# Moving the mLSTM's projections into the RWKV stage and running both scan halves beside the mLSTM

## The chip, the cores and the metric

The kernel runs on one core of a Trainium2 chip. The core's engines are TensorE (PE in the profile; its weight loads are listed apart as PEld), VectorE (DVE), ScalarE (ACT) and GpSimd (POOL); SyncE (SP) only issues transfers. The program gives each engine a queue of instructions of its own. The metric is the device time of one execution in microseconds (us). Lower is better.

## The reference

Two layers of a diffusion transformer work on 1280 tokens (256 of context, 1024 latent) of 1024 features. Each layer modulates a normalised input by vectors of a conditioning input, runs a mixer, projects its output back and ends with an MLP of 4096 hidden features. The change is in the mixer of the first ("even") layer, which joins an mLSTM and an RWKV-7 recurrence:

```python
mod = (silu_c @ ada_w[l] + ada_b[l])[:, None, :]
...
hj = jnp.concatenate([modulate(rmsnorm(xc, norm_g[l, 0]), shc_a, scc_a),
                      modulate(rmsnorm(x, norm_g[l, 0]), sh_a, sc_a)], axis=1)
...
mq, mk, mv, mo, mg, rfeat = split_cols(hj @ w_in, EV_SIZES)
qk = two_seq(lambda t: centred_dwconv(t, ml_conv), jnp.concatenate([mq, mk], axis=-1), n_ctx)
...
hm = mlstm_chunkwise(z(hd(q, ML_DIM)), z(hd(k, ML_DIM)), z(hd(mv, ML_DIM)), z(ig_fw, ig_bw), z(lf_fw, lf_bw))
y_ml = head_rmsnorm(dir_merge(hm, B, n_ctx), ml_norm) * jax.nn.sigmoid(mo.astype(f32))
rfeat = two_seq(lambda t: t + (neighbour_mean(t) - t) * rw_mu, rfeat, n_ctx)
r, k, v, wl, al, gl = split_cols(rfeat, (...))
...
y = rwkv7_scan(z(r), z(decay[0], decay[1]), z(key_d[0], key_d[1]), z(v), z(-kk), z(icl[0], icl[1]))
y_rw = y.reshape(B, T, RW_WIDTH) * (jax.nn.sigmoid(gl.astype(f32)) @ rw_g2)
out = jnp.concatenate([y_ml, y_rw], axis=-1).astype(dt)
```

`mq`, `mk` (512 features each) go through a convolution over three tokens; `mv` and `mo` (512 each) are the mLSTM's values and output gates; `mg` are 16 gate columns. `rfeat` are 1920 RWKV features, each mixed with its two neighbours in time. Both recurrences run forwards and backwards, and the two directions are added.

## The kernel before

All matmuls of projections are made of three with split operands (`mm3`, lines 288 to 291: high x high, low x high, high x low), eight along the contraction, so 24 for a run of up to 512 columns. `wsplit` (line 278) loads a block of weights on SP (line 283), copies its high part on ScalarE (284) and makes the low part on VectorE or GpSimd (285).

The order of work is written with generators. `weave` runs several of them in rounds; a number beside each says how many steps it makes per round, and generators given as `behind` go along without being waited for. What is emitted sooner has priority, and the compiler puts each engine's queue into order from that and from the data.

The even layer has these stages:

1. Start: the input is normalised and transposed; the first group of modulation vectors is computed (`ada`, line 227: 16 weight tiles per group, matmul at 246). `hh` and `hl` keep the modulated input, transposed, in two parts.
2. `lowrank` for both halves of the tokens, then `rkv(0, 0)`: projections of RWKV features through `project` (734). It copies each PSUM run to `praw` (746), scales a second copy (747) and adds the neighbours on VectorE (751, 752).
3. Eight iterations over (feature tile, half): `prepare` of one (decays, keys, chunk matrices `AR` and `BK`, lines 799 to 926) woven at rate 3 with `rkv` of the next at rate 1. `behind` them run `inverses` (inverses of 32x32 blocks on GpSimd, 771 and 772) and `joins` (two products per block pair, 671 and 678, written by 683). In the eighth iteration no `rkv` is left, and `conv` projects and convolves the 8 features of `mq` and `mk` (699 to 720).
4. Scan half 0 (`scan(0, d)`, two of the four feature tiles, both directions), woven at rate 1 with `dense` at 0.45, and `adas` behind at 0.85. `dense` (947 to 986) projects `mv`, `mo` and `mg` by token tiles: 4 column blocks of 260 by 10 token tiles; its outputs go by GpSimd's queue to memory. `adas` computes the other five groups of modulation vectors of both layers.
5. The mLSTM's gates (1194 to 1275): a chain of small instructions on all engines, written out before the next weave.
6. Scan half 1 at rate 1, the mLSTM of both directions (`mlstm`, 1287 to 1378) at 1.1, the rest of `adas` at 1.5, then `outs` (the output projection, which starts when both mLSTM directions are over and, tile by tile, when the scans have passed), then the norms ahead of the MLP.

A scan step handles 128 tokens in two half-steps of 64. Each goes through TensorE and back four times: the old state's part of the right side (1089, 1090; copied by 1092), the product with the inverse (1097; copied by 1099 on VectorE and 1100 on ScalarE), the state's update (1108, 1109; 1111 to 1117) and the output (1128, 1130). `amat` makes the chunk matrices of the next step in between (1037, 1055). `finish` (1150 to 1171) normalises a tile that both directions have passed.

Later, in the odd layer, twelve feature tiles are projected by `od_run` (the loop starts at line 1458).

Of the kernel before, what the change touches and what calls it, by code (L numbers as in the profile page):

```python
# [17 lines left out]
P = 128  # L18
D = 1024
KD = 8  # L20
# [16 lines left out]
    ("qn", 2), ("kvn", 1),  # L37
# [13 lines left out]
def host_pack(i):  # L51
# [6 lines left out]
        _cols(f["rw_ln_b"][0]), _cols(f["hg_lb"]), _cols(f["mla_q_norm"][0]), _cols(f["mla_kv_norm"][0]),  # L58
    ], axis=1)

    grow = np.zeros((4, 2, P, 512), np.float32)
    for l in range(2):
        for w, (col, nrow, j0) in enumerate(((2048, 1, 0), (5120, 3, 2))):
            for j in range(2):
                for v in range(2):
                    p = 32 * (j0 + j) + v
                    grow[2 * l + w, 0, p] = f["ada_b"][l, col + 512 * j: col + 512 * (j + 1)]
                    grow[2 * l + w, 1, p] = f["norm_g"][l, nrow, 512 * j: 512 * (j + 1)]
# [86 lines left out]
def _body(tc, nc, I, out, dbg, stop, es):  # L155
# [71 lines left out]
    def ada(l, pool, groups, bufs=3, tag="px"):  # L227
        for g in groups:
            ws = []

            def load(i):
                k, c0 = i % KD, 256 * (i // KD)
                w = pool.tile([P, 4, 256], F32, tag="adaw", name=nm("adaw"), bufs=bufs)
                SY.dma_start(w, I["ada_w"][l, k * P:(k + 1) * P, g * 2048:(g + 1) * 2048]
                             .rearrange("p (j c) -> p j c", j=4)[:, :, c0:c0 + 256])
                ws.append(w)
            for i in range(bufs):
                load(i)
            for hf in range(2):
                c0 = 256 * hf  # L240
                pr = ps(tag=tag)
                for k in range(KD):
                    yield
                    w = ws.pop(0)
                    for j in range(4):
                        TE.matmul(pr[32 * j:32 * (j + 1), 0:256], sc[:, k, :], w[:, j, :], start=k == 0, stop=k == KD - 1)
                    if KD * hf + k + bufs < 2 * KD:
                        load(KD * hf + k + bufs)
# [6 lines left out]
                ab = pc(f"adab{l}", 16 * g, 16).rearrange("p (j i) -> p j i", j=4)[:, :, 2 * hf:2 * hf + 2]  # L255
                mv = modT[:, l, 16 * g:16 * (g + 1), :].rearrange("p (j i) v -> p j i v", j=4)[:, :, 2 * hf:2 * hf + 2]
                for v in range(2):
                    V.tensor_tensor(mv[:, :, :, v], ptv[:, :, :, v], ab, op=ALU.add)
                if g >= 1:
                    w = g - 1  # L260
                    j0 = 0 if w == 0 else 2
                    for i, op in enumerate((ALU.add, ALU.mult)):
                        gr = pool.tile([P, 256], F32, tag="gr", name=nm("gr"), bufs=1)
                        SY.dma_start(gr, I["grow"][2 * l + w, i, :, c0:c0 + 256])
                        V.tensor_tensor(mr, mr, gr, op=op)
                    for j in range(2):
                        p0 = 32 * (j0 + j)
                        S.dma_start(grd[2 * l + w, :, 512 * j + c0:512 * j + c0 + 256], mr[p0:p0 + 2, :])
# [281 lines left out]
    mod_ = dram([T, 512], "mod_")  # L550
# [17 lines left out]
    with ExitStack() as ph:  # L568
# [4 lines left out]
        lay.enter_context(psum(ps=3, px=5))  # L573
# [3 lines left out]
        feats = [2064 + P * f for h in range(2) for f in (12, 13, 14)] + \  # L577
            [2064 + P * f for ft, h in order for f in (4 + ft, ft, 8 + ft)] + [P * f for f in range(8)]
# [53 lines left out]
        W = H + 4  # L632

        PART = (((0, 256, 1), (256, 386, 258)), ((638, 322, 0), (960, 320, 322)))
        SEG = (((0, 1, 256), (256, 258, 384)), ((0, 2, 640),))
        ZERO = ((0, 257), (642,))
        KEEP = (((0, 0, 256), (256, 0, 384)), ((0, 2, 320), (320, 0, 320)))
# [61 lines left out]
        def conv(f, wts, pool, tag):  # L699

            wh, wl = wts()
            for h in range(2):
                raw = pool.tile([P, W], F32, tag="praw", name=nm("praw"), bufs=1)
                for z in ZERO[h]:
                    V.memset(raw[:, z:z + 1], 0.0)
                for t0, n, r0 in PART[h]:
                    pt = ps()
                    for k in range(KD):
# [1309 lines left out]
```

## Time and profile before

| what | us |
|---|---|
| three runs | 4082.84, 4089.72, 4089.75 (median 4089.72) |
| the profiled execution | 4080.55 |
| its span, first to last instruction | 4078.4 |
| first scan copy (line 1092) and last | 671.1 and 1407.5 |
| first and last matmul of modulation (line 246) | 10.5 and 1019.0 |
| TensorE busy | 3720.3 (91% of the span) |
| VectorE busy | 2434.3 (60%) |
| ScalarE, GpSimd busy | 1369.7, 1401.2 (34% each) |

How to read it: the span is one execution; a row of a table by stage gives the stretch, its length, and for each engine the busy time and the number of instructions, then the granted TensorE clock as a share of full speed, the mean busy share of the 16 DMA engines, and GB/s. Matmuls overlap in the records, so a stretch with TensorE busy all the time need not have it at full pace. A row of the timeline gives start, length, engine, line, operation, tiles written and read, shape and count; in brackets stands the idle time before it and what ended it. In a row of groups the figures behind the bar are the busy time and the mean duration in ns, then the idle time ahead of it. In a row on one line or tile, three durations in ns are the least, the median and the greatest.

### The profile page before, as it was taken

How to read it: one execution, taken by the hardware profiler on the slowest of the kernel's cores; microseconds unless marked ns; L12 is line 12 of the kernel's file. 1: busy time of each engine (PE TensorE's matmuls, PEld its weight loads, DVE VectorE, ACT ScalarE, POOL GpSimd, SP SyncE). 2: the span in 40 equal slices, each digit the busy share in tenths (PEclk: the TensorE clock that was granted, in tenths of full speed). 3: DMA queues.
4: the chain of work that ended last, by engine and by line, in shares of the span. 5: the costliest groups of instructions: out<-in, count | busy, mean ns of one | idle time of the engine just before them, and what ended most of it. 6: DMA issues, size and time to landing. Idle time of an engine off the chain costs nothing. (4 is left out here: it accounts for less than half of the span.)

```text
span 4078.4 us, 68232 instructions
## 1 busy us (share of the span) xinstructions
PE 3720.3 (91%) x27052; PEld 3157.0 (77%) x27052; DVE 2434.3 (60%) x4387; ACT 1369.7 (34%) x2739; POOL 1401.2 (34%) x1404
## 2 busy tenths in 40 slices
PE   5988898998887989999999989998888979999998
PEld 3867687776776778999899979986666757888887
DVE  5587753443786545656655662228888466666665
ACT  3554422333344443221412143123343434223221
POOL 3055570111122244323433231233444445333332
PEclk7998998999797899999999999998999989999999
DMA  5456665778574442222322235222221354334332
GB/s 168 117 134 165 147 154 144 222 226 237 179 238 148 138 154 83 88 78 73 119 78 78 75 97 172 90 95 70 84 66 48 124 177 138 110 97 135 102 95 77
DMA packets 594776, 511.97 MB, mean 126 GB/s; under 512 B 161145, under 2 KB 521529, under 8 KB 594457
## 3 DMA queue, kind: packets, MB, share of 16 engines
q1 hardware_dynamic: 485928, 425.06, 35.8%
q10 hardware_dynamic: 97824, 48.28, 4.1%
q0 software_dynamic: 10704, 34.28, 2.3%
q8 instruction: 213, 3.49, 0.4%
q14 instruction: 107, 0.87, 0.1%
HBM read 391.59 MB, written 115.92 MB: 124 GB/s over the span
## 5 line engine op out<-in xcount | busy, mean ns | idle before, releaser
L284 ACT CAST wh<-raw 128x1024 fp32r<-128x1024 f32 x322 | 332.8, 1050 | 1019.6 <-PE ps L291 501.3
L291 PE MATMUL ps<-mh,wl 128*128 128x320 f32 (+3 forms) x1888 | 625.2, 331 | 5.8 <-POOL wl L285 5.7
L289 PE MATMUL ps<-mh,wh 128*128 128x320 f32 (+3 forms) x1888 | 625.8, 332 | 2.6 <-DVE acc L506 1.7
L290 PE MATMUL ps<-mh,wh 128*128 128x320 f32 (+3 forms) x1888 | 625.2, 331 | 0.7 <-POOL mh L341 0.7
L473 DVE TENSOR_TENSOR relu<-relu 128x320 f32<-128x320 f32 (+1 forms) x192 | 326.5, 1701 | 386.1 <-ACT relu L472 386.1
L285 POOL TENSOR_TENSOR wl<-raw,wh 128x1024 fp32r<-128x1024 f32 x145 | 353.8, 2440 | 585.1 <-ACT wh L284 585.1
L289 PE MATMUL ps<-wh,h1h 128*128 128x512 f32 x1152 | 450.8, 392 | 5.4 <-ACT acc L504 2.7
L506 DVE TENSOR_TENSOR acc<-ps,acc 128x512 f32<-128x512 f32 x540 | 359.1, 684 | 152.8 <-PE ps L291 150.4
L290 PE MATMUL ps<-wl,h1h 128*128 128x512 f32 x1152 | 449.7, 390 | 0.0
L291 PE MATMUL ps<-wh,h1l 128*128 128x512 f32 x1152 | 448.9, 390 | 0.0
L475 POOL TENSOR_TENSOR h1l<-relu,h1h 128x320 fp32r<-128x320 f32 (+1 forms) x192 | 206.5, 1076 | 495.4 <-DVE h1h L474 492.0
L291 PEld LDWEIGHTS ps<-mh,wl 128*128 128x128 f32 x1888 | 355.1, 188 | 27.2 <-POOL wl L285 7.0
L289 PEld LDWEIGHTS ps<-mh,wh 128*128 128x128 f32 x1888 | 355.4, 188 | 25.2 <-DVE acc L506 2.9
L290 PEld LDWEIGHTS ps<-mh,wh 128*128 128x128 f32 x1888 | 355.4, 188 | 22.2 <-POOL mh L341 1.0
L285 DVE TENSOR_TENSOR wl<-raw,wh 128x1024 fp32r<-128x1024 f32 x177 | 226.6, 1305 | 105.6 <-ACT wh L284 105.4
L289 PEld LDWEIGHTS ps<-wh,h1h 128*128 128x128 f32 x1152 | 216.7, 188 | 51.4 <-ACT acc L504 3.9
L289 PE MATMUL ps<-hh,wh 128*128 128x256 f32 (+3 forms) x736 | 241.3, 328 | 15.8 <-ACT r L747 4.9
L291 PE MATMUL ps<-hh,wl 128*128 128x256 f32 (+3 forms) x736 | 237.7, 325 | 19.6 <-DVE wl L285 19.3
L291 PEld LDWEIGHTS ps<-wh,h1l 128*128 128x128 f32 x1152 | 216.7, 188 | 45.7
L290 PEld LDWEIGHTS ps<-wl,h1h 128*128 128x128 f32 x1152 | 216.7, 188 | 43.4 <-DVE wl L285 0.2
L290 PE MATMUL ps<-hl,wh 128*128 128x256 f32 (+3 forms) x736 | 238.9, 325 | 5.4 <-POOL hl L630 5.1
L289 PEld LDWEIGHTS ps<-hh,wh 128*128 128x128 f32 x736 | 145.3, 197 | 25.2 <-issue 6.5
(536 smaller groups left out, 7916.3 us busy)
## 6 DMA issues: line engine op xcount, KB each, us to landing
raw<-in_mlp_w SPq DMA_DIRECT2D x256, 512.0 KB
adaw<-in_ada_w SPq DMA_DIRECT2D x96, 512.0 KB
raw<-in_ev_w SPq DMA_DIRECT2D x38, 512.0 KB
ard<-AR SPq DMA_DIRECT2D x32, 320.0 KB
bkd<-BK ACTq DMA_DIRECT2D x16, 640.0 KB
CM<-ard SPq DMA_DIRECT2D x80, 128.0 KB
BK<-bkd SPq DMA_DIRECT2D x40, 256.0 KB
qk<-qkd SPq DMA_DIRECT2D x20, 512.0 KB
```

The source lines that it names most:

```text
L284: S.copy(h, raw)
L285: (leng or G).tensor_tensor(l, raw, h, op=ALU.subtract)
L289: TE.matmul(o, lh, rh, start=first, stop=False)
L290: TE.matmul(o, lh, rl, start=False, stop=False)
L291: TE.matmul(o, ll, rh, start=False, stop=last)
L473: V.tensor_tensor(r_, r_, r_, op=ALU.mult)
L475: G.tensor_tensor(l_[:, t0:t0 + step], r_, a[:, t0:t0 + step], op=ALU.subtract)
L506: V.tensor_tensor(acc[i][:, cs_], pt, acc[i][:, cs_], op=ALU.add)
```

## The change

1. **Fillers.** `dense` is gone. The values (`v`), output gates (`o`) and convolved features (`c`) become 16 `filler` generators by feature tile. They are spread over the eight iterations of stage 3: 0, 1, 2, 1, 2, 1, 2 and 7. The gate columns become `gatecols`. `lowrank(1)` moves from ahead of the loop into its first iteration, beside `gatecols`. `prepare` runs at rate 1.6 in place of 3. Output gates are now kept feature-major (`mod_`).
2. **Neighbour mixing from PSUM.** `project` and the convolution share `mixed`: no copy to `praw`; ScalarE scales the middle and VectorE adds both neighbours straight from PSUM. PSUM is divided 4 and 4 in place of 3 and 5.
3. **`AR`** has two planes in place of three and is made in one instruction for all partitions; its write has three transfers in place of two.
4. **Scan.** Stages 4 to 6 become one weave: each direction runs scan half 0 and then half 1; the gates are a generator (`gates_ml`) beside it; the mLSTM waits for it and runs at 0.55, the modulation at 0.6.
5. **Modulation.** Groups 1 and 2 of the second layer move from `adas` to the loop of `od_run`, one step after each run. `ada` now loads 1024 neighbouring columns in place of 4 x 256.
6. **mLSTM's end.** The product with norm weight and output gate is made after the transposition, on VectorE (4 instructions), in place of one multiplication on GpSimd and one on VectorE before it and a copy on ScalarE after it.

```diff
-                w = pool.tile([P, 4, 256], F32, tag="adaw", name=nm("adaw"), bufs=bufs)
-                SY.dma_start(w, I["ada_w"][l, k * P:(k + 1) * P, g * 2048:(g + 1) * 2048]
-                             .rearrange("p (j c) -> p j c", j=4)[:, :, c0:c0 + 256])
+                w = pool.tile([P, 1024], F32, tag="adaw", name=nm("adaw"), bufs=bufs)
+                SY.dma_start(w, I["ada_w"][l, k * P:(k + 1) * P, c0:c0 + 1024])
...
-        lay.enter_context(psum(ps=3, px=5))
+        lay.enter_context(psum(ps=4, px=4))
...
+        fill = [("v", f) for f in range(4)] + [("o", f) for f in range(4)] + [("c", f) for f in range(8)]
+        meant = [0, 1, 2, 1, 2, 1, 2, 7]
...
+        def plain(wh, wl, t0, n):
+            pt = ps()
+            for k in range(KD):
+                mm3(pt[:, :n], wh[:, k, :], wl[:, k, :], hh[:, k, t0:t0 + n], hl[:, k, t0:t0 + n], k == 0, k == KD - 1)
+                if k == 3:
+                    yield
+            return pt
+
+        def mixed(h, wh, wl, o_, left, mid, right):
+
+            for t0, n, o0, p0, m, nl, nr in PART[h]:
+                pt = yield from plain(wh, wl, t0, n)
+                S.activation(o_[:, o0:o0 + m], pt[:, p0:p0 + m], AF.Copy, scale=mid)
+                o = o_[:, o0 + nl:o0 + m]
+                V.scalar_tensor_tensor(o, pt[:, p0 - 1 + nl:p0 - 1 + m], left, o, op0=ALU.mult, op1=ALU.add)
+                o = o_[:, o0:o0 + m - nr]
+                V.scalar_tensor_tensor(o, pt[:, p0 + 1:p0 + 1 + m - nr], right, o, op0=ALU.mult, op1=ALU.add)
+                yield
+
+        def filler(y, f):
+
+            wh, wl = weights()
             for h in range(2):
...
+                o_ = ep.tile([P, H], F32, tag="fo", name=nm("fo"), bufs=2)
+                if y == "c":
+                    yield from mixed(h, wh, wl, o_, *[cw[:, j, f:f + 1] for j in range(3)])
+                    by_tile(qkd[5 * h:5 * h + 5, :, f, :], o_)
+                    continue
+                for c0, nn in ((0, 3), (3, 2)):
+                    w = slice(c0 * P, (c0 + nn) * P)
+                    pt = yield from plain(wh, wl, H * h + c0 * P, nn * P)
+                    if y == "o":
+                        S.activation(o_[:, w], pt[:, :nn * P], AF.Sigmoid)
+                        yield
+                        continue
+                    S.copy(o_[:, w], pt[:, :nn * P])
...
+        def gatecols():
...
+            for t in range(NT):
+                o, tk = pt[:, 32 * t:32 * t + 32], slice(t * P, (t + 1) * P)
+                for k in range(KD):
+                    TE.matmul(o, hh[:, k, tk], gw[:, k].rearrange("p y g -> p (y g)"), start=k == 0, stop=False)
+                for k in range(KD):
+                    TE.matmul(o[:, 0:16], hl[:, k, tk], gw[:, k, 0], start=False, stop=k == KD - 1)
...
-                    for p0 in (0, 64):
-                        q = slice(p0, p0 + 64)
-                        V.tensor_tensor(to(AR[q, :, p0 // 32, w]), half_(kn)[q], dec(Wq)[q], op=ALU.mult)
+                    V.tensor_tensor(to(AR[:, :, 0, w]), half_(kn), dec(Wq), op=ALU.mult)
...
-        weave(chain(lowrank(0), lowrank(1)))
+        weave(lowrank(0))
...
-            gens = [(prepare(ft, h, cur["k"], cur["r"], cur["v"]), 3, 0)]
+            feed = [] if i else [lowrank(1), gatecols()]
             if i + 1 < len(order):
-                gens.insert(0, rkv(*order[i + 1], res))
-            else:
-                gens.insert(0, chain(*[conv(f, weights, ep, "k") for f in range(8)]))
+                feed.append(rkv(*order[i + 1], res))
+            feed += [filler(*next(fl_)) for _ in range(meant[i])]
+            gens = [chain(*feed), (prepare(ft, h, cur["k"], cur["r"], cur["v"]), 1.6, 0)]
...
-                for l, gs in ((0, (1, 2)), (1, (0, 1, 2))):
+                for l, gs in ((0, (1, 2)), (1, (0,))):
...
-        weave((dense(), 0.45, 0), (scan(0, 1), 1, 0), (scan(0, 0), 1, 0), behind=((mods, 0.85, 0),))
...
         def mlstms(d):
+            while not pre:
+                yield
...
         def scans1(d):
+            yield from scan(0, d)
             yield from scan(1, d, got[0])
...
-        weave((mlstms(1), 1.1, 0), (scans1(1), 1, 0), (mlstms(0), 1.1, 0), (mods1(), 1.5, 0), (norms0(), 3, 0), (scans1(0), 1, 0), (outs(), 1, 0))
+        weave((gates_ml(), 1, 0), (mlstms(1), 0.55, 0), (scans1(1), 1, 0), (mlstms(0), 0.55, 0), (mods1(), 0.6, 0), (norms0(), 3, 0), (scans1(0), 1, 0), (outs(), 1, 0))
...
+        mods = ada(1, epx.enter_context(tc.tile_pool(name="ad1", bufs=1, reuse_waits="tile")), (1, 2), 3, "ps")
...
                 pt = held.pop(1) if f == F0 and r in runs[:2] else od_run(w, *r)
+                next(mods, None)
```

More of the change, by code (lines that the diff above doesn't have):

```diff
@@ L549, in _body @@
     mvd = dram([T, 512], "mvd")
-    mod_ = dram([T, 512], "mod_")
+    mod_ = dram([NT, P, 4, P], "mod_")
     und = dram([640, 32, 32], "und")
@@ L576, in _body, with rw @@
         order = [(ft, h) for ft in range(4) for h in range(2)]
-        feats = [2064 + P * f for h in range(2) for f in (12, 13, 14)] + \
-            [2064 + P * f for ft, h in order for f in (4 + ft, ft, 8 + ft)] + [P * f for f in range(8)]
+        fill = [("v", f) for f in range(4)] + [("o", f) for f in range(4)] + [("c", f) for f in range(8)]
+        meant = [0, 1, 2, 1, 2, 1, 2, 7]
+        col = {"v": 1024, "o": 1536, "c": 0}
+        def rw(fs):
+            return [2064 + P * f for f in fs]
+        feats = rw((12, 13, 14)) + rw((4, 0, 8)) + rw((12, 13, 14))
+        for i, n in enumerate(meant):
+            if i + 1 < len(order):
+                ft = order[i + 1][0]
+                feats += rw((4 + ft, ft, 8 + ft))
+            at = sum(meant[:i])
+            feats += [col[y] + P * f for y, f in fill[at:at + n]]
         ready = []
@@ L736, in project @@
             wh, wl = weights()
[L737 to L752 removed]
+            yield from mixed(h, wh, wl, o_, half[:, f:f + 1], omu[:, f:f + 1], half[:, f:f + 1])
         def rkv(ft, h, res):
@@ L791, in lowrank @@
                 o_ = ep.tile([P, H], F32, tag="kn", name=nm("gg"), bufs=1)
+                g2 = ep.tile([P, 2, P], F32, tag="lr", name=nm("g2"), bufs=2)
+                SY.dma_start(g2[:, 0, :], I["rw_g2"][:, ft * P:(ft + 1) * P])
                 for t0, n in HC:
                     pt = px()
-                    TE.matmul(pt[:, :n], g2[:, ft * P:(ft + 1) * P], sgl[:, t0:t0 + n], start=True, stop=True)
+                    TE.matmul(pt[:, :n], g2[:, 0, :], sgl[:, t0:t0 + n], start=True, stop=True)
                     S.copy(o_[:, t0:t0 + n], pt[:, :n])
@@ L884, in prepare @@
                     yield
-                for p0 in (0, 64):
-                    q = slice(p0, p0 + 64)
-                    SY.dma_start(ard[d][tiles, q, ft].rearrange("c p s t -> p c (s t)"),
-                                 AR[q, :, p0 // 64:p0 // 64 + 2, :].rearrange("p c s t -> p c (s t)"))
+                SY.dma_start(ard[d][tiles, 0:64, ft].rearrange("c p s t -> p c (s t)"), AR[0:64].rearrange("p c s t -> p c (s t)"))
+                for s_ in range(2):
+                    SY.dma_start(ard[d][tiles, 64:128, ft, s_].rearrange("c p t -> p c t"), AR[64:128, :, 1 - s_, :])
                 S.dma_start(bkd[d][tiles, :, ft].rearrange("c p e s t -> p c (e s t)"), BK.rearrange("p c e s t -> p c (e s t)"))
@@ L1396, in outs @@
         def outs():
-            while over.count("m") < 2:
+            while over.count("m") < 2 or not mdone:
                 yield
@@ L1482, in _body @@
                 by_tile(fkd[d][:, :, 1, h, :], b_)
+        for _ in mods:
+            pass
         epx.close()
```

335 lines of the change are left out of this document (145 added, 190 removed).

## The prediction

> **What bounds the kernel now.** I read the page's slices first, then a table of busy times by stage, then one line of the scan by stage.
>
> ```profile
> span 4078.4 us, 68232 instructions
> PE   5988898998887989999999989998888979999998
> PEclk7998998999797899999999999998999989999999
> ```
>
> TensorE has work nearly everywhere and the clock is nearly full; the dips stand in the first 15 slices of 102 us, before the first MLP. The change edits just that stretch, so I cut it where its stages change.
>
> ```profile
> core 0: us, PE busy (x) PEld busy (x) DVE busy (x) ACT busy (x) POOL busy (x), PEclk, DMA share, GB/s
> 62.00:165.00 103.00, 85.26 (x493) 77.51 (x494) 58.32 (x92) 46.79 (x87) 20.90 (x12) 0.88 0.32 87
> 165.00:484.00 319.00, 264.96 (x1986) 227.06 (x1985) 253.09 (x418) 153.77 (x270) 151.95 (x205) 0.91 0.60 148
> 484.00:660.00 176.00, 160.99 (x1269) 150.09 (x1267) 85.14 (x140) 56.91 (x106) 96.41 (x151) 0.94 0.55 132
> 660.00:1001.00 341.00, 317.89 (x3705) 249.96 (x3705) 147.44 (x480) 108.38 (x284) 55.03 (x85) 0.92 0.78 225
> 1001.00:1054.00 53.00, 38.33 (x287) 27.73 (x285) 22.66 (x87) 17.73 (x39) 3.16 (x9) 0.55 0.52 156
> 1152.00:1287.40 135.40, 117.30 (x1320) 99.73 (x1318) 109.19 (x345) 56.38 (x208) 33.88 (x39) 0.91 0.64 194
> 1054.00:1285.00 231.00, 197.55 (x2059) 169.45 (x2057) 184.97 (x575) 96.44 (x335) 56.68 (x65) 0.91 0.66 202
> 1285.00:1465.00 180.00, 150.12 (x998) 115.25 (x999) 91.89 (x216) 79.91 (x159) 51.71 (x38) 0.84 0.45 143
> 2368.00:2580.00 212.00, 200.65 (x1297) 193.92 (x1297) 86.58 (x101) 75.21 (x151) 53.56 (x36) 0.98 0.44 133
> ```
>
> The rows are: low-rank projections; seven of the eight RWKV iterations; the eighth, with the convolutions; scan half 0 beside `dense`; the mLSTM gates; scan half 1 beside the mLSTM, first the later part and then the whole; scan half 1 beside the output projection; and far behind, the first projections of the odd layer. The two middle kinds differ. In 165 to 484 VectorE is busy 79% and TensorE 83%, a mixture in which neither is full. From 660 to 1465, 805 us, the work is a recurrence that is cut into half-steps, and `L1092` runs once per half-step and direction:
>
> ```profile
> core 0: us, DVE busy (x), PEclk, DMA share, GB/s
> 660.00:1001.00 341.00, 11.25 (x40) 0.92 0.78 225
> 1001.00:1054.00 53.00, 0.64 (x3) 0.55 0.52 156
> 1152.00:1287.40 135.40, 4.74 (x18) 0.91 0.64 194
> 1054.00:1285.00 231.00, 6.67 (x26) 0.91 0.66 202
> 1285.00:1465.00 180.00, 3.25 (x12) 0.84 0.45 143
> ```
>
> Half 0 takes 341/20 = 17.05 us a half-step, half 1 with the mLSTM 231/13 = 17.8 (135.4/9 = 15.0 once its first loads are over). The gates' 53 us hold the recurrence up almost wholly.
>
> **What the scan pays for its neighbour.** One half-step of half 0, as a whole, then `dense` in it, then the modulation:
>
> ```profile
> 908.00:925.00 17.00, 16.91 (x204) 13.65 (x206) 11.18 (x35) 7.27 (x15) 0.54 (x1) 1.00 0.83 229
> 908.00:925.00 17.00, 6.29 (x48) 5.88 (x48) 0.00 (x0) 0.00 (x0) 0.00 (x0) 1.00 0.83 229
> 908.00:925.00 17.00, 3.04 (x28) 0.93 (x32) 1.00 0.83 229
> ```
>
> TensorE looks full, but 9.3 of its 17 us are the two guests. How much lies on the path is seen in the order of time:
>
> ```profile
> 916.36 0.26 ACT L1100 COPY ZV<-ps 64x128 f32<-64x128 f32 x1 [4.53 <-DVE ZV L1099]
> ...
> 917.75 0.28 PE L291 MATMUL ps<-wt,hl 128*128 128x260 f32 x1
> 917.96 0.27 PE L1108 MATMUL ps<-ZV,KB 128*64 128x64 f32 x1
> ...
> 921.20 0.39 PE L289 MATMUL ps<-wt,hh 128*128 128x260 f32 x1
> ...
> 924.06 0.28 PE L291 MATMUL ps<-wt,hl 128*128 128x260 f32 x1
> 924.27 0.27 PE L1089 MATMUL ps<-ZV,CM 128*64 128x64 f32 x1
> ```
>
> The update `L1108` could start when `L1100` ends (916.62) and starts at 917.96: 1.3 us behind a block of `dense`. The next half-step's `L1089` waits out a whole block, 921.20 to 924.27: 3.1 us. So 4.4 of 17.05 us go with `dense`, which leaves 12.6; I take 12.7.
>
> **Part by part. Stage with the fillers (62 to 660).** Added on TensorE: eight features (values, gates) of 4 runs x 24 matmuls, 320 columns in the mean, and 160 matmuls for the gate columns, each with a load of 128 columns.
>
> ```profile
> 240.65 0.31 PE L289 MATMUL ps<-hh,wh 128*128 128x322 f32 x1
> ...
> 241.38 0.30 PE L291 MATMUL ps<-hh,wl 128*128 128x322 f32 x1
> ...
> 40.13 0.93 PEld L609 LDWEIGHTS ps<-cm,xt 128*128 128x128 f32 x8 [0.81 <-DVE xT L611]
> ```
>
> Five steps in 0.73 us give 0.146 us a matmul; eight loads in 0.93 us give about 0.113 each. Added: 768 x 0.146 + 160 x 0.113 = 112 + 18 = 130 us. The convolutions keep their 8 features. What hides the 130 is the idle part of the iterations:
>
> ```profile
> 165.00:484.00 319.00, 112.27 (x338) 66.93 (x338) 0.91 0.60 148
> ```
>
> `L289` is one of three, so 1014 projection matmuls in seven iterations: 145 each, 21 us, and the other (1986 - 1014)/7 = 139 I put at 10 us, an estimate below 139 x 0.113 = 16, since most load 64 columns and fewer. So 31 of 319/7 = 45.6 us per iteration. A filler adds 96 x 0.146 = 14. By the plan (0, 1, 2, 1, 2, 1, 2, 7 fillers, and low-rank half 1 with the gate columns in the first) TensorE needs about 75 (31 + 24 + 18), three times 45, three times 59, and in the last 10 + 98 + 12 for joins: 507. How full can it be? 83% in this row, 95% in the odd projections (200.65 of 212); with fillers always ready I take 90%: 563 us. Ahead lie the start up to about 75, one low-rank half (30) and the first projection (25). End: 693 against 660, **+33**. Bounds: at 95% +4; nothing hidden, +130. VectorE does not take over:
>
> ```profile
> L880 DVE TENSOR_TENSOR AR<-kn,Wp 64x320 f32<-64x320 f32 x64 | 41.7, 652 | 1.3 <-DMA ard<-AR 0.7
> L746 ACT COPY praw<-ps 128x256 f32<-128x256 f32 (+3 forms) x60 | 25.6, 426 | 111.9 <-DVE k L752 44.7 <-DVE r L752 24.1 <-PE ps L291 18.3
> L772 POOL TENSOR_TENSOR xu<-xu,tm 128x31 f32<-128x31 f32 (+15 forms) x155 | 112.6, 727 | 12.2
> L771 POOL TENSOR_TENSOR tm<-un,xu 128x31 f32<-128x31 f32 (+15 forms) x155 | 104.5, 674 | 37.9 <-DMA un<-und 26.1
> L683 ACTq DMA_DIRECT2D xcd<-XC x16: 366/401/754, 336.8 to 666.7; - x16
> ```
>
> `AR` is made in 32 whole pieces and not 64 halves: 21 us of VectorE go, about as much as the fillers' weight splits bring. The `praw` copies go from ScalarE; in their place VectorE now reads PSUM, so a bank comes free only when VectorE has passed, which a fourth bank eases; I cost that at nothing, and at up to 5 us an iteration if VectorE is late. The fillers' writes, two a feature, leave by ScalarE's queue, each waiting for the last pass over its tile; behind it stand the activations of `prepare`. The convolutions' writes do that already, and `dense`'s 50 small writes leave GpSimd's queue. The inverses are 217/5 = 43 us each on GpSimd; the last follows the last `prepare`, then come joins (before, the last was written at 666.7). The last iteration's 120 us cover an inverse and most joins; 15 us may show, within the bounds.
>
> **Both scan halves beside the mLSTM (660 to 1465 before).** Gone: `dense`, the serial gates, the gap between the halves. The mLSTM runs at 0.55 and not 1.1, so its 59 steps of the generator per direction last 107 rounds, after 8 for the gates: 115 of the scans' 174 rounds (87 per half). That is 26.5 of 40 half-steps; 13.5 remain. Price of a half-step in the first part: 12.7 with no neighbour, 15.0 with a full mLSTM, hence about 13.9 with half of one; 14.0 with a little modulation. VectorE's share fits: at most 147.44/20 = 7.4 us of scan and half of (109.19 - 9 x 7.4)/9 = 4.7 of mLSTM, 10 of 14. The part is 26.5 x 14.0 = 371. The rest: before, 180 us from 1285 to the MLP held 7 half-steps, the one in hand counted; 6.5 more beside weight splits alone, at 13.5, are 88. The first loads and the mLSTM's start take 20, an estimate (the mLSTM's first loads cost 231 - 13 x 15.0 = 36 in half 1). Sum 659 against 805: **-146**. Bounds: a price of 12.7 gives -180, one of 16.9 gives -50; above that the first rival holds. A new wait is the hand-over: half 1's first loads stand on SP behind half 0's last; mLSTM work covers one landing.
>
> **Modulation.** Layer 1's last two groups, 32 weight tiles, move into the odd projections, with their loads on SP and small writes on ScalarE's queue.
>
> ```profile
> 660.00:1001.00 341.00, 55.19 (x584) 13.57 (x584) 0.92 0.78 225
> L246 PE MATMUL ps<-adaw,sc x768: 376/403/637, 10.5 to 1019.4; 128*32 128x256 f32 x192
> ...
> PE ps L246 <- DMA adaw<-in_ada_w: 15.0, 5, 10.5
> ```
>
> 768 records are 96 tiles of 8; 584 are 73, at 0.76 us busy, less where matmuls overlap. 32 tiles are 24 us at most, 0 if they fell into the 11 us that TensorE is idle there. That stage is full (200.65 of 212), so I take **+17**. The od weights' loads stand behind them on SP; three buffers ahead cover a landing. The last row is of the waits up to 62 us: TensorE waits 15.0 us for such loads, 10.5 of it for the first. Whole rows of 1024 columns in place of four pieces can shorten the other 4.5: **-2**, between 0 and -4.
>
> **Sum.** -2 + 33 - 146 + 17 = -98. The profiled execution took 4080.55 us (span 4078.4), 9 under the median of the three runs, 4089.72. From it 3982.5; with half of those 9, 3987.
>
> **Rivals.** (Each with the same half of 9.)
> *The scan is paced by its own hops.* PE, VectorE and ScalarE hand each half-step on several times, in queues in order; taking `dense` away may only show other waits (in the rows above ScalarE sat 4.53 us behind VectorE's `L1099`, not behind `dense`). Place: `L1099` to `L1108`. If a half-step keeps the 17.8 of half 1 in the 33 of them that I price anew, 33 x 17.8 + 180 + 20 = 787, -18 and not -146; with 33 + 17 - 2 the kernel is 30 us slower: 4115. It decides from 16.9 us on, where 33 c + 200 is 805 - 48. For it: 17.05 and 17.8 have different neighbours and nearly one price. Against: 15.0 in the nine half-steps with a full mLSTM, where VectorE is 81% busy and so has reason to be the pace. Chance 0.11.
> *The scan runs free.* The mLSTM hides wholly: 33 x 12.7 + 180 + 12 = 611, -194, and fillers at +4: 3910. For it: `L1089` follows `dense` by 0.2 us, so it was ready. Against: VectorE is not idle. Chance 0.19.
> *A colder array.* The clock was granted 0.55 where the gates ran alone and 0.84 beside the output projection. Without `dense` the recurrence might see 0.75 and not 0.91: TensorE's 16.91 - 9.33 = 7.6 us of scan and half of (117.30 - 9 x 7.6)/9 = 5.4 of mLSTM, 10.3 a half-step, grow by 2.2, over 33 of them 72: 4059. Against it, 1054 to 1285 has no `dense` and 0.91. Chance 0.14. The Trainium skill (TensorE: Matmul & The Clock Gate, Part 1: The HAM clock gate) speaks for this rival: an idle window of some 3.4 us brings the array to half rate, and busy time brings it back. The row of 0.55 agrees; the row of 0.91 says that the mLSTM is work enough.
> *The fillers hide nothing*, since banks wait for VectorE or the order leaves them last: the first stage grows by 130, not 33: 4084, no change. For it: VectorE is 79% busy there. Against: TensorE's 17% idle. Chance 0.08.
>
> **Numbers.** Forecast 0.48, then 0.11, 0.19, 0.14, 0.08 in the order above. The range runs from 3905 (free scan) to 4075 (colder array with the fillers one fifth less hidden); the hop-paced case and most of the last stay outside. A difference under 0.2%, 8 us, cannot be told from none here. Faster 0.83, same 0.06, slower 0.11.
>
> **What would show it.** Right: scans start near 693; about 14 us between `L1092` pairs until the mLSTM ends, no hole between the halves; the MLP starts some 100 us sooner; the odd projections last about 229 us. Wrong: a clock under 0.8 in the scans, pairs over 16 us apart, scans starting after 740, or odd projections longer by over 25 us.

## The result, and the profile after

The changed kernel takes 4183.57 us (median of 4 runs, 4179.2 to 4188.22); the kernel before took 4089.12 beside it (4082.84 to 4089.75). The ratio is 1.0235, 95% interval 1.0217 to 1.0252: 94 us slower, where 103 us less was forecast and the range ended at 4075. The page of the changed kernel, by the lines with which the prediction began:

```profile
span 4178.1 us, 67908 instructions
PE   5997788888888889999999989998888879999998
PEclk7898899989888889999999999998989989999999
```

TensorE's thin part ends with slice 15 in both kernels, but from slice 4 on it no longer has a slice at 9, where it had four (6, 8, 9 and 14). Cut by stage (the columns are those of the prediction's tables), first the kernel before: filler stage, both scan stages up to the first matmul of the MLP, first projections of the odd layer, rest.

```profile
62.00:660.00 598.00, 511.21 (x3744) 454.66 (x3744) 396.54 (x648) 257.47 (x461) 269.26 (x368) 0.91 0.54 133
660.00:1494.00 834.00, 729.13 (x7153) 582.81 (x7153) 458.33 (x1374) 310.93 (x835) 175.51 (x206) 0.88 0.64 193
...
2413.00:2581.00 168.00, 159.31 (x1081) 158.33 (x1080) 56.96 (x60) 63.37 (x130) 43.75 (x26) 0.98 0.50 146
2581.00:4078.00 1497.00, 1383.56 (x9779) 1122.84 (x9777) 937.13 (x1529) 478.09 (x900) 584.76 (x546) 0.97 0.32 101
```

The same stages after the change:

```profile
59.00:840.00 781.00, 651.75 (x4774) 602.85 (x4776) 363.98 (x638) 260.14 (x444) 244.35 (x375) 0.88 0.48 119
840.00:1552.00 712.00, 595.92 (x5870) 458.55 (x5870) 421.37 (x1316) 288.11 (x773) 112.32 (x123) 0.86 0.59 182
...
2468.00:2669.00 201.00, 188.54 (x1348) 167.82 (x1346) 63.01 (x78) 64.47 (x130) 43.08 (x26) 0.97 0.67 208
2669.00:4178.00 1509.00, 1389.74 (x9777) 1128.40 (x9776) 936.72 (x1529) 479.45 (x900) 582.54 (x546) 0.96 0.32 100
```

The stage with the fillers ends at 840 and not 660 (+180). The scan stages take 712 and not 834 (-122), the odd projections 201 and not 168 (+33), the MLP 916 and not 919. The rest holds the same work and takes 1509 and not 1497; between two fixed matmuls of it (its first with `wt` and `mh`, and the last of all) lie 1479 to 1493 us in the twenty kernels of this study, so these 12 are within that scatter. The sum is 100, as the spans say. Two things stand out. TensorE is busy 141 us more in the first stage (651.75 against 511.21), and it is also idle 42 us more (129 against 87): nothing has been hidden, and something new waits. In the iterations with one filler and with two, in turn, it shows:

```profile
234.00:285.00 51.00, 46.00 (x354) 41.95 (x353) 27.09 (x53) 21.90 (x40) 9.32 (x18) 1.00 0.60 145
285.00:386.00 101.00, 74.88 (x556) 68.42 (x556) 39.34 (x62) 31.45 (x57) 36.95 (x51) 0.85 0.44 108
386.00:438.00 52.00, 49.46 (x398) 44.82 (x397) 30.55 (x57) 24.59 (x44) 15.19 (x28) 1.00 0.63 153
438.00:535.00 97.00, 70.83 (x529) 65.96 (x529) 39.18 (x61) 28.00 (x48) 57.97 (x86) 0.84 0.47 117
535.00:606.00 71.00, 57.57 (x445) 52.09 (x446) 35.45 (x62) 25.93 (x45) 18.77 (x24) 0.90 0.52 128
606.00:689.00 83.00, 64.98 (x522) 60.40 (x522) 38.19 (x71) 26.76 (x47) 40.13 (x68) 0.90 0.52 133
```

The first two iterations with one filler take 51 and 52 us, as planned (45 at 90%, 50); the first two with two fillers take 101 and 97 (66 planned), with TensorE idle for 26. The third of each kind takes 71 and 83. The timeline of the second row, on GpSimd, SP and TensorE (`L811` writes an inverse, `L662` loads it for a join, `L280` loads weights):

```profile
314.88 0.30 PE L288 MATMUL ps<-hh,wl 128*128 128x322 f32 x1
...
323.31 0.61 POOL L811 DMA_DIRECT2D xud<-xu  x1
...
326.39 0.33 SPq L662 DMA_DIRECT2D XC<-xud  x1
326.81 0.63 SPq L280 DMA_DIRECT2D raw<-in_ev_w  x1
...
332.36 0.69 PE L286 MATMUL ps<-hh,wh 128*128 128x384 f32 x1 [17.17 <-ACT wh L281]
```

SP's queue goes in order. A load that waits for an inverse stands ahead of the next weights; they leave 0.4 us after it, and TensorE, which has run out of weights, waits 17.17 us. One more wait like it comes in the next iteration with two fillers; together they are the costliest wait of TensorE between 138 and 840, where it is idle for 112 us in all:

```profile
PE ps L286 <- ACT wh L281: 33.4, 2, 17.2
```

SP's own waits in that time:

```profile
SPq L662 <- DMA xud<-xu: 141.1, 5, 34.0
SPq L659 <- PE ps L676: 50.6, 11, 9.6
SPq L280 <- DVE wl L282: 48.5, 15, 6.8
```

Five waits for an inverse, 141 us in all. The kernel before has one in this stage, 14.8 us for `xtd`.

### The profile page after: what moved, and what is told of

It is laid out like the page before. It is cut to its first block, busy times and chain, and to the rows that moved or that the text cites. A ratio compares the mean times of both kernels' runs of the same rounds, so it can differ in the third digit from the quotient of the medians.

```text
span 4178.1 us, 67908 instructions
## 1 busy us (share of the span) xinstructions
PE 3759.9 (90%) x27060; PEld 3195.6 (76%) x27060; DVE 2369.7 (57%) x4335; ACT 1351.3 (32%) x2658; POOL 1308.6 (31%) x1328
## 3 DMA queue, kind: packets, MB, share of 16 engines
q1 hardware_dynamic: 459160, 424.01, 34.5%
## 5 line engine op out<-in xcount | busy, mean ns | idle before, releaser
L281 ACT CAST wh<-raw 128x1024 fp32r<-128x1024 f32 x330 | 341.8, 1051 | 1089.8 <-PE ps L288 493.7
L286 PE MATMUL ps<-hh,wh 128*128 128x256 f32 (+2 forms) x992 | 328.4, 331 | 37.0 <-ACT wh L281 33.4
L282 DVE TENSOR_TENSOR wl<-raw,wh 128x1024 fp32r<-128x1024 f32 x185 | 235.9, 1299 | 205.6 <-ACT wh L281 203.6
L288 PE MATMUL ps<-hh,wl 128*128 128x256 f32 (+2 forms) x992 | 316.2, 319 | 11.1 <-DVE wl L282 11.1
L287 PE MATMUL ps<-hl,wh 128*128 128x256 f32 (+2 forms) x992 | 317.9, 320 | 5.3 <-POOL hl L639 5.0
L286 PEld LDWEIGHTS ps<-hh,wh 128*128 128x128 f32 x992 | 195.3, 197 | 45.4 <-ACT wh L281 33.9
```

Of the source, the lines that this page charges most:

```text
L281: S.copy(h, raw)
L282: (leng or G).tensor_tensor(l, raw, h, op=ALU.subtract)
L286: TE.matmul(o, lh, rh, start=first, stop=False)
L287: TE.matmul(o, lh, rl, start=False, stop=False)
L288: TE.matmul(o, ll, rh, start=False, stop=last)
```

## The experiments

Each ratio is to the kernel before, run beside it on the same chip; the changed kernel stands at 1.0235. A thousandth is 4.1 us. "End" is the end of the filler stage (the last join or projection): 829 in the changed kernel, 665 before.

| kernel | ratio, 95% interval | end | MLP starts |
|---|---|---|---|
| e1_gq: joins' loads on GpSimd's queue | 1.0098 (1.0077 to 1.012) | 775 | 1505 |
| e2_late: joins later in the program | 1.0195 (1.0168 to 1.0221) | 816 | 1541 |
| e3_end: fillers all at the end | 1.0126 (1.01 to 1.0151) | 791 | 1523 |
| e4_mods: modulation back | 1.024 (1.0218 to 1.0263) | 819 | 1580 |
| e5_gates: gate columns turned | 1.0186 (1.0162 to 1.021) | 804 | 1537 |
| e6_ones: e1, one filler per iteration | 1.0134 (1.0117 to 1.0151) | 783 | 1516 |
| e7_both: e6 and e5 | 1.0052 (1.0036 to 1.0069) | 759 | 1485 |
| e8_rate: e7, preparation at rate 3 | 1.0157 (1.0133 to 1.0182) | 799 | 1529 |
| e18_fill4: half of the fillers at a quarter | 1.0179 (1.0165 to 1.0193) | 804 | 1528 |
| e13_fewloads: modulation weights, a quarter loaded | 1.0161 (1.0135 to 1.0187) | - | 1518 |
| *on the kernel before:* e9_gates_in | 1.0015 (0.9998 to 1.0033) | - | 1491 |
| e10_dense4: `dense` at a quarter | 1.0068 (1.0045 to 1.0092) | - | 1526 |
| e14_d4_fewloads: e10, a quarter of the loads | 0.975 (0.9732 to 0.9768) | - | 1388 |
| e11_mixed: the RWKV stage's own edits | 0.9986 (0.9969 to 1.0003) | - | 1491 |
| e12_two: e9 and e11 | 0.9987 (0.9972 to 1.0002) | - | - |
| e15_one, e16_one_b: one scan stage with `dense` | 1.0117 (1.0099 to 1.0134), 1.009 (1.0071 to 1.0108) | - | 1537, 1529 |
| e17_mods_early | 1.0022 (1.0012 to 1.0031) | 700 | 1497 |

**Who holds SP.** The first theory was that SP's waits alone make the stage long.

```diff
-                SY.dma_start(XT[64 * e:64 * e + 32], xtd[us]...
+                G.dma_start(XT[64 * e:64 * e + 32], xtd[us]...
...
-                SY.dma_start(XC[32 * q:32 * q + 32, :, ...
+                G.dma_start(XC[32 * q:32 * q + 32, :, ...
```

> The joins' loads of XT and XC (lines 660 and 662) are issued on GpSimd's queue, behind the inverse that they wait for, in place of SP's. Theory A (SP's queue alone is the cause: five of its waits for xud, 31.1 + 34.0 + 20.2 + 28.6 + 27.3 = 141 us, hold back the weight loads queued behind them): the filler stage ends near 740 in place of 840 and the kernel takes about 4085. Rival B (the joins stand too early in every queue): TensorE then waits at line 676 for XT, some 20 us each time, with the projections behind that matmul; about 30 us are won, 4155. Rival C (TensorE has no room for the fillers, the weights come in time): within 15 us of 4184.

The kernel comes out 56 us below the changed one, between A and B. The iterations with two fillers:

```profile
285.00:366.00 81.00, 71.94 (x556) 66.21 (x555) 41.00 (x62) 31.01 (x55) 50.68 (x69) 0.96 0.54 134
...
419.00:497.00 78.00, 69.54 (x527) 65.31 (x525) 40.47 (x60) 26.93 (x45) 60.52 (x89) 0.91 0.55 141
```

The wait for `xud` is gone from SP, and 20 us of each of these iterations with it. They stop at 81 and 78, though, and not at 66, because TensorE is busy 72 and 70 in them. What is left is mostly work, as rival C has it. B's wait of TensorE for `XT` is 8.2 us at the longest. SP is not free of waits, though: `L659`, another load of the joins, now waits 135 us for TensorE, where it waited 51, so a part of the rest may still be SP's order. The Trainium skill (DMA: Bandwidth & Descriptors, Issuing engines are not separate DMA queues) says that issuing from several engines saves only the usually small time to initiate a transfer. Here it saved more than that: the issuer itself waited up to 34 us for what it was to send, and the second queue was worth 56.

```diff
-                while P * inverted[0] < 40 * (i + 1):
+                g = (40 * i + 39) // P
+                while len(born) <= g or ticks[0] < born[g] + EXTRA[g]:
```

> Each join is put later in the program, by some 12 more steps of the joins' generator after its inverse has been written out (15 more rounds of the weave; 7 for the fourth inverse, none for the last), all transfers on SP as in the changed kernel; the inverses follow one another without the pause of 7 rounds. Theories A and B: SP's waits for xud fall under 5 us each, the iterations with two fillers take about 66 us and not 83 to 101, the kernel about 4085 (100 us less), less what joins left to the end of the stage add, up to 20. Rival C: within 15 us of 4184.

A miss: 16 us less. The first load of `XC` stays where it was, behind the same wait, though it stands 12 steps later in the program:

```profile
SPq L662 <- DMA xud<-xu: 30.3, 1, 30.3
```

So the place in the program doesn't set SP's order here; the compiler's planning does. That it takes the inverse for faster than it is would fit, and is only argued.

```diff
-        meant = [0, 1, 2, 1, 2, 1, 2, 7]
+        meant = [0, 0, 0, 0, 0, 0, 0, 16]
```

> All 16 fillers run in the last iteration (0 in the first seven). Rounds per iteration are 12 again, as before the change, so the joins stand as far behind their inverses as they did there. Theories A and B: no waits of SP for xud over 10 us in the first seven iterations, which take about 46 us each from the second on; the last takes 16 x 14 + 22 at 95%, 260; the stage ends near 775, the kernel takes about 4120. Rival C: the fillers cost their whole TensorE time wherever they stand, stage end 840, 4184. A fourth outcome, slower than 4200, would say that what little the fillers hid in the middle iterations was worth more than the waits.

```profile
268.00:518.00 250.00, 211.51 (x1556) 179.11 (x1556) 175.24 (x284) 105.98 (x176) 158.98 (x228) 0.89 0.65 156
518.00:800.00 282.00, 265.51 (x2018) 256.68 (x2016) 89.62 (x140) 71.41 (x134) 75.39 (x120) 0.97 0.45 117
```

With nothing spread, the kernel is 45 us faster than with the plan: the little that the fillers hid was worth less than the waits that they brought. SP's only long wait for an inverse is then one of 18.2 us, for `xtd`. The five iterations of the first row are 50 us each with no filler, and the last one takes 282 us, 22 more than expected: TensorE is busy 265.5 in it.

**TensorE's own time.** Is the stage's TensorE work what one sees in the end? The gate columns were turned round (weights loaded, tokens streamed):

```diff
-                    TE.matmul(o, hh[:, k, tk], gw[:, k]..., start=k == 0, stop=False)
+                    TE.matmul(pt[0:32, :320], gw[:, k]..., hh[:, k, 320 * r:320 * r + 320], start=k == 0, stop=False)
```

> The changed kernel, with the gate columns turned round: the 32 columns of the gates' weights are loaded and 320 tokens stream past them (64 matmuls), and ten small transposes bring the result back, where the changed kernel loads 128 tokens at a time for 32 or 16 columns that stream (160 matmuls, which took from 165 to 201 us with the granted clock at 0.65 and then 0.54). Theory (TensorE has no slack in this stage, so its time shows in full, and the narrow matmuls cool the array as well): 64 matmuls at 0.146 to 0.163 us are about 10, so the stretch of 36 us shrinks by some 25 and the kernel by 25, 4159. Rival (they lay beside work that sets the pace): within 8 us of 4184.

First the changed kernel, then the experiment, the same 36 us by the clock:

```profile
165.00:183.00 18.00, 18.00 (x91) 16.24 (x91) 0.68 (x3) 4.54 (x10) 0.00 (x0) 0.65 0.57 132
183.00:201.00 18.00, 18.00 (x92) 18.00 (x92) 0.61 (x2) 0.00 (x0) 0.00 (x0) 0.54 0.27 65
```

```profile
165.00:183.00 18.00, 18.00 (x119) 12.63 (x116) 1.75 (x6) 7.93 (x17) 0.00 (x0) 1.00 0.87 206
183.00:201.00 18.00, 18.00 (x125) 18.00 (x124) 8.85 (x14) 6.59 (x11) 0.00 (x0) 1.00 0.45 118
```

20 us less; the stage ends 25 sooner, as expected. The columns gate reads: TensorE is busy without a gap in both, but with 32 columns streaming per load of 128 the granted clock is 0.65 and 0.54, with 320 columns it is 1.00. The Trainium skill (TensorE: Matmul & The Clock Gate, Part 1: The HAM clock gate) has busy time release the throttle; these rows do not agree with it, if busy is what the profile counts as busy.

The opposite test leaves out six of eight products in the fillers of values and gates:

```diff
-                    pt = yield from plain(wh, wl, H * h + c0 * P, nn * P)
+                    pt = yield from plain(wh, wl, H * h + c0 * P, nn * P, (0, 4))
```

> The changed kernel, in whose fillers of values and output gates six of the eight products along the contraction are left out (their sums are incomplete): 576 matmuls of 320 columns fewer in the filler stage, with every load, split and write kept. If TensorE's time binds that stage: 576 x 0.163 = 94 us less, 1.0005 of the kernel before. If SP's waits for the inverses hold the stage whatever TensorE does: the 94 us go only outside of them, 30 to 60 less, 1.009 to 1.016. If the array cools as well, still less.

```profile
59.00:800.00 741.00, 593.32 (x4133) 536.18 (x4134) 367.31 (x605) 252.28 (x432) 247.46 (x350) 0.84 0.49 121
```

```profile
SPq L662 <- DMA xud<-xu: 126.9, 4, 39.6
```

Only 23 us go for 94 of matmuls. SP's waits stay (the second fence), and the clock falls to 0.84, so that even TensorE's busy time falls only from 652 us to 593: busy time at a lower clock is not the same amount of work. So the stage has two limits at nearly one height: take either away and the other is met within 20 to 60 us.

**How the fillers are spread.** e6 puts one filler in each iteration and ten in the last, on e1; e7 adds the turned gate columns; e8 has the preparation at rate 3 again.

> The joins' loads on GpSimd's queue as in the first experiment (which ran 57 us below the changed kernel), and the fillers spread 0, 1, 1, 1, 1, 1, 1, 10. Iterations with one filler took 51 to 53 us where those without took 36 to 56 and those with two 67 to 81, so six with one filler are some 312 from 234, to 546; the last, with ten fillers at 15.4 us and 57 for its own work and the joins, 211: stage end 757 in place of 780, 23 us less than the first experiment. Rival (only the sum of TensorE's work counts, wherever it stands): no difference from the first experiment.

> Joins' loads on GpSimd's queue, one filler per iteration and ten in the last, and the gate columns turned round. If the three add up, -57 - 23 - 25 = -105 from the changed kernel: 0.998 of the kernel before. If the gate columns and the rest share the same waits, 1.003 to 1.01.

> The kernel with all three edits, and the preparation of each iteration at rate 3 in place of 1.6, as before the change. If the preparation comes too late at 1.6 and its writes hold up the inverses, 10 to 30 us less than with 1.6; if fillers and projections have to come first, as much more; if the compiler's own order decides, within 8 us.

e6 is a miss: 15 us slower than e1, not 23 faster; the iterations with one filler take 55 to 78 us, but for the first (53). e7 gains 34 more and is the best of the changed kernels, still 21 us behind the kernel before. e8 loses 43. Why the later iterations are long in e6, and why rate 3 costs so much, is not settled.

**Modulation.**

```diff
-                for l, gs in ((0, (1, 2)), (1, (0,))):
+                for l, gs in ((0, (1, 2)), (1, (0, 1, 2))):
```

> The last two modulation groups of layer 1 stay in the scan stage, as before the change; the odd projections run without them. The odd projections took 201 us in the changed kernel and 168 before. If the scan stage takes the 32 weight tiles for nothing (TensorE idle 116 us of 712 there): 33 us less, 4151. If they cost there what TensorE needs for them, 24 us at most: 4175. If the odd projections do not grow shorter, their 33 us have another cause: 4184 or more.

```profile
830.00:1580.00 750.00, 614.64 (x6137) 458.73 (x6137) 423.76 (x1334) 285.79 (x770) 111.86 (x125) 0.85 0.63 196
...
2497.00:2667.00 170.00, 162.10 (x1078) 161.54 (x1077) 56.36 (x59) 62.95 (x129) 43.48 (x26) 0.97 0.49 144
```

The odd projections get 31 us back, and the scan stage, which here begins at 830, gives 38 away (750 in place of 712); the first stage happens to end 10 sooner. A tie: the move costs nothing and brings nothing. TensorE is idle for 135 of those 750 us, so 38 us for at most 24 of matmuls say that something other than TensorE paces it.

**What paces the scan.** The forecast had `dense` hold up each half-step of scan half 0 by 4.4 us. Three quarters of its matmuls were left out of the kernel before, loads and writes kept:

```diff
-                            mm3(pt[:, :n], a, b, ...)
+                            if k % 4 == 0:
+                                mm3(pt[:, :n], a, b, ...)
```

> The kernel before, with six of the eight products along the contraction left out of dense (its sums are incomplete), so 720 of its 960 matmuls of 260 columns, with its loads, splits and writes kept: what does the guest cost scan half 0? By the prediction's reading of one half-step, all of dense holds 4.4 of 17.05 us, three quarters of it 3.3: half 0 takes 275 us in place of 341, the kernel 66 less. If TensorE's time is the bound there, 720 x 0.122 = 88 us go. If the recurrence's own hops pace it, under 20.

```profile
667.00:1006.00 339.00, 261.00 (x2888) 183.36 (x2886) 144.97 (x467) 108.30 (x281) 54.42 (x83) 0.76 0.70 209
```

339 us where the kernel before has 341: `dense` held up nothing. The kernel is even 28 us slower, most of it later, beside the mLSTM (249 us where 230 were, clock 0.86 and not 0.91); that part stays open. Hops, clock or transfers? The next two load only every fourth weight tile of the modulation in the scan stages, with all its matmuls:

```diff
             def load(i):
+                if tag == "mo" and i % 4:
+                    ws.append(ws_[0])
+                    return
```

> The kernel before with three quarters of dense's matmuls left out, as in the tenth experiment, and every fourth of the modulation's weight tiles loaded in the scan stages. Half 0 then moves some 29 MB less of 77. Transfers pace the scan: half 0 falls from 339 us to between 215 and 265. The recurrence's hops pace it: 320 to 340, at whatever clock. The clock does: it falls below 0.76, and half 0 takes 340 or more.

```profile
667.00:905.00 238.00, 222.79 (x2925) 156.11 (x2926) 146.12 (x473) 103.86 (x278) 54.35 (x84) 0.93 0.65 192
```

238 us for 20 half-steps (40 copies of the right side lie in it), 11.9 each, at a clock of 0.93. So the modulation's loads paced the stage once `dense` was gone. They could do so in two ways, which no run takes apart: by their bytes (the stage moved 209 GB/s at a DMA share of 0.70 in e10 and 192 at 0.65 here), or by holding SP's queue, on which the scan's own loads stand too. Ahead of a load of modulation weights (`L234` in e10, `L237` here) SP waits above all until a matmul has freed the buffer; first e10, then this run:

```profile
SPq L234 <- PE ps L246: 41.5, 20, 7.0
```

```profile
SPq L237 <- PE ps L250: 6.3, 4, 3.1
```

With SP's other waits ahead of these loads it is 89 us of 339 and 7 of 238. The recurrence's own hops need no more than the 11.9 us, and the clock of 0.76 was a result of the waiting, not its cause. In the kernel before, both limits seem to have stood at one height: TensorE busy 318 of 341 us, DMA share 0.78. No run leaves out the loads alone there, so that TensorE's work would then have held the stage is argued from these figures, not shown.

> The changed kernel, in whose scan stage only every fourth of the 48 modulation weight tiles is loaded (each serves four times, so the modulation is not the right one); the matmuls stay as many. 36 x 512 KB = 18.9 MB of the stage's 130 MB go. Transfers pace the scan: 18.9 MB at the stage's 245 GB/s are 77 us, 40 to 77 less than the changed kernel, 1.005 to 1.014 of the kernel before. Hops or clock pace it: within 10 us, 1.021 to 1.026.

Copies of the right side (two per half-step) up to the end of the mLSTM and after it, in the changed kernel and then in this one:

```profile
840.00:1270.00 430.00, 14.54 (x52) 0.87 0.70 213
1270.00:1552.00 282.00, 7.67 (x28) 0.85 0.43 134
```

```profile
840.00:1231.00 391.00, 14.41 (x52) 0.87 0.60 184
1231.00:1510.00 279.00, 7.74 (x28) 0.84 0.42 132
```

26 half-steps take 430 us and 391: 39 us belong to the modulation's loads, again by their bytes or by SP, which waited 41 us ahead of them in the changed kernel and not at all here. 30 show in the whole, fewer than the 40 to 77 of the expectation.

**Is the one stage worth anything?** e9 takes the gates alone into the weave of half 1; e15 and e16 make one scan stage with `dense` left in it; e11 has only the RWKV stage's own edits.

> The kernel before, with one piece of the change only: the mLSTM's gates (1001 to 1054 us, granted clock 0.55, the scans standing still) become a generator in the weave of scan half 1 in place of a block ahead of it. Fillers, dense, modulation and scan half 0 stay. Theory (the hole in the recurrence is the one part of this change that has idle TensorE time to win): half 1 does some three half-steps meanwhile, 35 to 50 us less: 4040 to 4055 where the kernel before takes 4089, 0.988 to 0.992. Rival (the mLSTM, which still has to wait for its gates, sets the end of the stage, since the output projection follows it): within 10 us.

> The kernel before with its scan stages made one and nothing moved out of them: one weave of both scan halves, in which dense comes first (0.8 of a step per round), then the gates, then the mLSTM (0.7), with all modulation at 0.6 and the output projection behind. The RWKV stage is the old one with its end at 660. If dense and the mLSTM are both nearly free beside the recurrence: 40 half-steps of 16 to 17 us and some 85 to the MLP, MLP at 1400 to 1440 and not 1494, 0.977 to 0.987 of the kernel before. If every guest costs the recurrence what TensorE needs for it, as the prediction had it: 40 x 12.7 + 117 + 26 x 5.4 + 85 = 850, no gain.

> The same with dense at 0.6 and the mLSTM at 0.9: the mLSTM starts some four half-steps later and runs faster, and would end after 67 + 8 + 66 of 174 rounds in place of 50 + 8 + 84. If the recurrence is the spine and guests are free, within 8 us of the kernel with 0.8 and 0.7; if the guests' crowding counts, 10 to 30 us slower.

> The kernel before, with the RWKV stage's own edits alone: neighbours mixed straight from PSUM, PSUM divided 4 and 4, AR in two planes with three writes; no fillers, preparation at rate 3. The prediction costed them at nothing, and at up to 5 us an iteration (40 in all) if VectorE is late in freeing banks. If the 21 us of VectorE that AR saves count where VectorE was 79% busy: 10 to 20 us less.

> The kernel before with the gates in the weave and the RWKV stage's own edits, the two experiments above in one. If both keep what they bring alone, the sum of the two: 35 to 60 us below the kernel before, 0.985 to 0.991. If the last joins and inverses on GpSimd set the end of the RWKV stage, the gates' part alone.

The hopes fall in all of them. In e9 the last copy of the scan comes at 1373 and not 1407, and the MLP starts at 1491 and not 1494: the rival is right, the output projection waits for the mLSTM, and that ends at 1294 and not 1281. The hole also stays: the longest stretch without a scan copy, between the halves, is 45 us and was 55. In e15 TensorE waits in the middle as it does everywhere:

```profile
900.00:1300.00 400.00, 319.50 (x3457) 240.33 (x3455) 251.50 (x819) 151.92 (x446) 54.87 (x82) 0.83 0.69 211
```

Beside the mLSTM the DMA share is 0.69 and VectorE is 63% busy. One stage is 37 to 48 us slower than two. e11 and e12 cannot be told from the kernel before: mixing from PSUM and the new `AR` cost nothing, as the prediction had it.

A last attempt, on top of e11's edits, lowered both limits of half 0 together: two groups of modulation moved into the RWKV stage.

```diff
+        behind = ((invs, 2, 0), (jns, 0.8, 0), (ada(1, ep, (1, 2), 1, "mo"), 0.3, 0))
```

> The kernel before with the RWKV stage's own edits (0.9986 alone), and the last two of layer 1's modulation groups (32 weight tiles, 16.8 MB, at most 24 us of TensorE) computed in the RWKV stage behind everything else, through one buffer, in place of the scan stage; PSUM 3, 4 and 1. Scan half 0 loses transfers and TensorE work together: 48 tiles at 0.55 in place of 73, so 13 MB of 77 and 19 us of 318 busy. Theory (two limits at one height, both lowered): half 0 takes 310 to 325 us in place of 341, the RWKV stage 5 to 20 more, the kernel 0.992 to 0.998. Rival (half 0 gives nothing, or the RWKV stage takes back all of it): 0.999 to 1.006.

```profile
62.00:665.00 603.00, 509.92 (x3762) 432.87 (x3762) 360.98 (x599) 225.09 (x367) 253.41 (x368) 0.90 0.61 157
665.00:1001.00 336.00, 320.97 (x3587) 262.47 (x3586) 151.65 (x467) 111.57 (x289) 52.88 (x80) 0.92 0.63 185
```

Half 0's first 40 copies come 18 us closer together (297 us, 315 before), but the first one comes at 704 and not 671: the RWKV stage took 33 for it, where 5 to 20 were expected. Of the versions that compute everything none beats the kernel before; e9, e11 and e12 tie with it.

## Why the prediction was wrong

- **The step that failed: "So 31 of 319/7 = 45.6 us per iteration", and the sum to 693 that stands on it.** The row quoted above it says that TensorE was busy 264.96 us in those seven iterations: 37.9 each. The 31 us were counted at full clock, where the row has 0.91, and the 10 us in them for everything but projections were too low; if busy time goes with the clock (an estimate: 37.9 x 0.91 = 34.5), each is about half of the miss. Idle were 7.7 us per iteration, not 14.6: 54 us in seven, for 130 of new work. With TensorE 85% busy, as it had been (511 of 598), 652 us of work need 762, which is +161 of the +180. In the prediction's own sum, the eight iterations were to keep TensorE busy 507 us, at 90%; they kept it busy 590 us of 702, at 84%, and began at 138 and not at 130. The 83 us more make 92 of the 147 us by which the end missed 693, the lower share 47, the start 8. The plan held where the clock was full (46 and 49 us busy with one filler, 45 planned) and not where it was 0.85 and 0.84 (75 and 71 with two, 59 planned).
- **A size within it:** the gate columns, put at 18 us, took 36 by the clock (165 to 201); turning them was worth 20. They are 18 of the 83 us.
- **A wait that was not costed:** weights stand on SP behind the joins' loads. The prediction named ScalarE's queue and left SP out of this stage. Taking the loads off SP was worth 56 us. It overlaps with the first point: e1, with those waits gone, still ends at 775.
- **The rival "the fillers hide nothing" (0.08) is what happened**, and its bound of +130 was too low, since it took the new matmuls at full clock and added no wait. It is right in its outcome alone: it blamed banks that wait for VectorE, or an order that leaves the fillers last. The profile lists no wait of a projection for a bank between 138 and 840, and the fillers ran spread out, as planned.
- **Scan stage, forecast -146, measured -122.** The sum is near, in part by luck: 26.5 half-steps were put at 391 us with the first loads, and 26 take 430; the rest takes 282, where 268 and the 29 us from 1465 to the MLP's first matmul make 297. There is no hole between the halves, and the clock (0.87, 0.85) stayed above 0.8. But the price of a half-step came from a wrong reading: 4.4 us of waiting behind `dense` in one half-step was taken for what `dense` costs. Without three quarters of it the stage is as long, since the modulation's loads stand right behind. That the stages still gain is no proof of the reading: `dense` left them, and its price is paid in the first stage.
- **Odd projections, forecast +17, measured +33.** A size (the prediction's row of 212 us takes in 45 us of the MLP; the stage itself had 168, at the same 95%): TensorE's busy time rose there by 29, where 24 at most were worked out from records of another stage. The same two groups would cost the scan stage 38 (e4), so the move itself is a tie; its other half lies in the -122.
- **Start -2:** 59 against 62 for the first projection; as forecast.
- Of the four signs of being wrong that were named, three came: scans after 740 (847), pairs over 16 us apart (16.5 in the first part), odd projections longer by over 25 us (33). The fourth, a clock under 0.8 in the scans, did not.

The account of the whole: TensorE is busy nearly as long up to the MLP in both kernels (1240 us before, 1248 after), and the change only moves work: it removes none but the modulation that goes behind the MLP, and finds no idle time for the rest. Before, 192 us were idle there; after, 245.

## What to carry to other kernels

A filler is free only in idle time that the busy column of its own stage shows; take that column first, at the clock that was granted there, and don't rebuild it from full-speed prices. A guest that seems to hold up a recurrence in the timeline costs what the stage loses without it: leave three quarters of it out and look, since a second limit may stand at the same height. Before more work is put into a stage, list what stands in each in-order queue behind a transfer that waits for a slow engine.

## What was not expected of the hardware

- TensorE busy without a gap can be granted 0.54 to 0.65 of its clock: 160 matmuls of 32 or 16 streamed columns with a load of 128 columns each. The same product with 320 streamed columns had 1.00 (e5).
- The granted clock followed the wait of the stage and did not cause it: with three quarters of `dense` gone scan half 0 had 0.76 and took as long as at 0.92; with three quarters of the modulation's loads gone too it had 0.93 and took 238 us.
